# A second set of raw-weight buffers in the MLPs, half of it in large slots, and another order of the weight splits

## The chip, the cores and the metric

The kernel runs on one core of one Trainium2 chip. The metric is the device time of one execution in microseconds; each time given is the median of several executions on one chip. The engines are TensorE (PE), VectorE (DVE), ScalarE (ACT), GpSimd (POOL) and SyncE (SP), whose queue issues nearly all of this kernel's DMAs. Each engine takes its instructions in order.

## The reference

A trunk of two layers over 1024 positions with 1024 channels, all in fp32. Layer 0 mixes with a chunked gating MLP, layer 1 with dilated attention; each is followed by an MLP with squared ReLU, four times as wide. Cut to what matters here:

```
D_MODEL, SEQ, D_FF = 1024, 1024, 4 * 1024
h = x
for layer in range(2):
    y = _rms_norm(h, mix_norm_g[layer])
    y = _chunk_gating_mixer(y, ...) if layer == 0 else _dilated_attention_mixer(y, ...)
    h = h + y
    y = _rms_norm(h, mlp_norm_g[layer])
    h = h + jnp.square(jax.nn.relu(y @ w_up[layer])) @ w_down[layer]
return _rms_norm(h, final_norm_g)
```

## The kernel before

**Precision.** A matmul in fp32 is made of three in fp32r. Each operand is split into a high part (ACT copies it with rounding, line 203) and a low part (DVE subtracts, line 204), and PE adds hi × hi, hi × lo and lo × hi in one bank (`three`).

**Seven products for eight.** The large matrix products are cut into 2 × 2 blocks and done with seven products in place of eight. The weights of one such set are four raw quadrants of 128 × 512 (`Weights`, line 370). They are loaded by SP into buffers with the tag "r", of which there are four. POOL makes the sums (lines 389, 390, 391, 394), partly in place in the raws, and seven splits (ACT and DVE) write `wp` tiles, of which there are eight. Which product uses what: 4 uses r(1,1) raw, 1 uses r(0,0), 2 uses r(0,1); 5, 6, 7 and 3 use sums. Two sets are thus never raw at the same time: the loads of the next set wait until the splits of the set before have read its raws.

**Stages.** An MLP has an up stage of tiles q = 2 to 15 (q = 0 and 1 are computed in the classical way), and a down stage of tiles t = 0 to 17. In both, PE computes products in the order 5, 6, 1, 7, 3, 2, 4, and the weights of the next tile are split meanwhile: after each product the generator `more()` goes one step on. A full product is 12 matmuls of 512 columns (four blocks of 128 rows, three matmuls each). The first and last three tiles of the down stage have fewer blocks: tile 0 has one, tile 1 two, tile 2 three. The first set of an up stage (q = 2) and of the attention has no tile before it to hide in and is split at one go (line 712).

**Around it.** Up tiles put out hidden terms, which go to DRAM (`hid`, line 669). The down stage loads them again one tile ahead, in temporary tiles `t`, and splits them into `hx` pairs (`take`, `inputs`). DVE adds products to the state `h` (line 833) and to the partial sums `u` (lines 847, 856, 859), and in the up stage combines banks (lines 739, 746, 747, 755). A product that begins in a bank which an earlier one has used (3, 2 and 4 continue in the banks of 5, 1 and 7, new tiles take freed ones) waits for that.

**Slots.** A pool of 38 slots of 128 × 1024 words holds the state (8), and, depending on the stage, normed activations, hidden terms as pairs, or raw hidden terms. The last block of hidden terms is done in the classical way at the end of the down stage, with weights `we` and terms `xe` that are loaded and split during its last tiles (`ends`).

**Order.** PE's order is as written. On the other engines a list scheduler sets the order from the program order, dependencies and priorities (`tc.high_priority`), so the change of one buffer can move other instructions as well.

Of the kernel before, what the change touches and what calls it, by code (L numbers as in the profile page):

```python
# [10 lines left out]
F32 = mybir.dt.float32  # L11
# [6 lines left out]
P = 128  # L18
D = 1024
S = 1024  # L20
HALF = 512
# [91 lines left out]
def trunk(ctx: ExitStack, tc: tile.TileContext, xT, w_u, w_v, w_o, w_s, b_s, w_qkv, w_bo, rel,  # L113
# [14 lines left out]
    def temp():  # L128
        return tpool.tile([P, HALF], F32, tag="t", name="t", bufs=NT)
# [7 lines left out]
    def slot(shape=(P, S), dtype=F32, name="s"):  # L137

        return slots.tile(list(shape), dtype, tag="s", name=name)
# [21 lines left out]
    def raw():  # L161
        return tpool.tile([P, HALF], F32, tag="r", name="r", bufs=4)
# [10 lines left out]
    def mm_bank():  # L173
        return psm.tile([P, HALF], F32, tag="mm", name="mm")

    def at_bank():
        return psa.tile([P, HALF], F32, tag="at", name="at")
# [186 lines left out]
    def product(bank, w, xs, more=False):  # L364

        for k, x in enumerate(xs):
            three(bank, w, blk(k), x, not more and k == 0, k == len(xs) - 1, skip_group_check=True)
            flow.pump()

    class Weights:  # L370


# [11 lines left out]
        def steps(self):  # L384

            r, tt = self.r, nc.gpsimd.tensor_tensor
            self.split(4, r[1, 1])
            r3 = temp()[:, 0:r[0, 0].shape[1]]
            tt(r3, r[0, 0], r[1, 0], op=ALU.subtract)  # L389
            tt(r[1, 0], r[1, 0], r[1, 1], op=ALU.add)  # L390
            tt(r[1, 1], r[1, 0], r[0, 0], op=ALU.subtract)  # L391
            yield
            self.split(1, r[0, 0])
            tt(r[0, 0], r[0, 1], r[1, 1], op=ALU.subtract)  # L394
            yield
            for p, src in ((5, r[1, 0]), (6, r[1, 1]), (7, r3), (3, r[0, 0]), (2, r[0, 1])):
                self.split(p, src)
                yield

# [12 lines left out]
    def up(layer, q):  # L412
        return lambda i, j: w_up[layer, q, i, j]
# [276 lines left out]
    def mlp(layer, x, first, last):  # L690


        def up_weights(q):
            return Weights(up(layer, q))


        tiles = [(q, i) for q in range(2) for i in range(2)]
        c = {}
        for s in range(2):
            banks = [at_bank() if (n < 2) == (s == 1) else mm_bank() for n in range(4)]  # L700
            if s == 0:
                banks = [mm_bank() if n < 3 else at_bank() for n in range(4)]
            classical(x, first, s, banks)
            for b, (q, i) in zip(banks, tiles):
                c[q, i, s] = temp()
                with tc.high_priority(offset=PRIO):
                    squared(c[q, i, s], b)
                if s and i:
                    hidden_terms(q, c[q, 0, 0], c[q, 1, 0], c[q, 0, 1], c[q, 1, 1], c[q, 0, 0])
            if s == 0:  # L710
                w = up_weights(2)
                for _ in w.steps():
                    pass
        x.rest()

        for q in range(2, 16):
            down = Down(layer) if q == 15 else None
            wn = down.weights(0) if down else up_weights(q + 1)
            more = ahead(wn)
            more()  # L720
            d = at_bank()
            product(d, w[5], x.t[5])
            more()
            c22 = temp()
            nc.scalar.activation(c22, d, AF.Copy)  # L725
            if down:
                down.take(14, held, SEVEN[:4])
            b = at_bank()
            product(b, w[6], x.t[6])
            more()  # L730
            if down:
                down.take(14, held, SEVEN[4:])
            a = mm_bank()
            product(a, w[1], x.t[1])
            more()
            u = temp()
            with tc.high_priority(offset=PRIO):
                nc.scalar.activation(u, a, AF.Copy)  # L738
                nc.vector.tensor_tensor(u, u, b, op=ALU.add)
            if down:  # L740
                down.early(SEVEN[:4])
            e = at_bank()
            product(e, w[7], x.t[7])
            more()
            with tc.high_priority(offset=PRIO):
                nc.vector.tensor_tensor(c22, c22, e, op=ALU.add)  # L746
            nc.vector.tensor_tensor(c22, c22, u, op=ALU.add)
            squared(c22)
            if down:
                down.early(SEVEN[4:])  # L750
            product(d, w[3], x.t[3], True)
            more()
            c12 = temp()
            with tc.high_priority(offset=PRIO):
                nc.vector.tensor_tensor(c12, u, d, op=ALU.add)
            squared(c12)
            product(a, w[2], x.t[2], True)
            more()
            c11 = temp()
            squared(c11, a)  # L760
            product(e, w[4], x.t[4], True)
            more()
            c21 = temp()
            with tc.high_priority(offset=PRIO):
                nc.vector.tensor_tensor(c21, u, e, op=ALU.add)
            squared(c21)
            if q < 14:
                hidden_terms(q, c11, c21, c12, c22, u)
            elif q == 14:
                held = hidden_terms(q, c11, c21, c12, c22, u, False)  # L770
            else:
                kept(q, {(0, 0): c11, (1, 0): c21, (0, 1): c12, (1, 1): c22})
            w = wn
        down.run(w)
        down.close(last)

    class Down:
# [41 lines left out]
        def run(self, w):  # L819
            for t, (a, ks) in enumerate(self.todo):  # L820
                hs = {(i, s): h[a + 4 * i][:, half(s)] for i in range(2) for s in range(2)}
                wn = None
                if t < 17:
                    wn = self.weights(t + 1, **(dict(own=temp, place=pair) if t == 16 else {}))
                more = ahead(wn)
                more()

                def xs(p):
                    return [self.x[self.order[k]][p] for k in ks]

                def add(i, s, src, engine=nc.vector):
                    with tc.high_priority(offset=PRIO if engine is nc.vector else 0):
                        engine.tensor_tensor(hs[i, s], hs[i, s], src, op=ALU.add)  # L833

                if t == 16:
                    self.ends(0)
                d = at_bank()
                product(d, w[5], xs(5))
                more()
                add(1, 1, d)  # L840
                self.inputs(t + 1, (5,))
                b = at_bank()
                product(b, w[6], xs(6))
                more()
                if t >= 4:
                    with tc.high_priority(offset=PRIO):
                        nc.vector.tensor_tensor(self.u[a], self.u[a], b, op=ALU.add)
                self.inputs(t + 1, (6,))
                a_ = mm_bank()
                product(a_, w[1], xs(1))  # L850
                more()
                if t < 4:
                    self.u[a] = spare() if t < 2 else temp()
                    with tc.high_priority(offset=PRIO):
                        nc.scalar.activation(self.u[a], a_, AF.Copy)
                        nc.vector.tensor_tensor(self.u[a], self.u[a], b, op=ALU.add)
                else:
                    with tc.high_priority(offset=PRIO):
                        nc.vector.tensor_tensor(self.u[a], self.u[a], a_, op=ALU.add)  # L859
                self.inputs(t + 1, (1,))  # L860
                if t == 16:
                    self.ends(1)
                e = at_bank()
                product(e, w[7], xs(7))
                more()
                add(1, 1, e)
                self.inputs(t + 1, (7,))
                product(d, w[3], xs(3), True)
                more()
                add(0, 1, d)  # L870
                if t >= 14:
                    for i, s in ((1, 1), (0, 1)):
                        add(i, s, self.u[a], nc.gpsimd)
                self.inputs(t + 1, (3,))
                product(a_, w[2], xs(2), True)
                more()
                add(0, 0, a_)
                self.inputs(t + 1, (2,))
                product(e, w[4], xs(4), True)
                more()  # L880
                add(1, 0, e)
                if t >= 14:
                    add(1, 0, self.u[a], nc.gpsimd)
                self.inputs(t + 1, (4,))
                w = wn
# [531 lines left out]
    for n, two in enumerate(quads):  # L1417
        wn = Weights(qkv(*quads[n + 1])) if n + 1 < len(quads) else None
# [123 lines left out]
```

## Time and profile before

| | us |
|---|---|
| time, median of 3 runs | 2202.07 (2201.95 to 2205.04) |
| the profiled execution | 2201.35 |
| its span | 2199.6 |
| PE busy | 2129.9 |
| DVE busy | 1664.0 |
| ACT busy | 1132.7 |
| POOL busy | 608.3 |
| mean granted clock of PE | 0.987 |

The down stages run from about 626 to 930 and from about 1863 to 2170, the up stages from about 352 and 1592 on. A row of the timeline gives start, length, engine, line, operation, written and read tiles, shape and count; in brackets stands how long the engine was idle before it, and who ended that.

### The profile page before, as it was taken

What the parts mean: (1) busy time and instruction counts of PE and PEld (TensorE: products, weight loads), DVE (VectorE), ACT (ScalarE), POOL (GpSimd) and SP (SyncE); (2) the same over time, 40 slices, a digit from 0 to 9 for tenths busy, and PEclk for the clock granted to TensorE, in tenths of its full rate; (3) what the DMA queues carried; (4) which work ended last, traced back from release to release, by engine and by line L of the source; (5) the groups of instructions that cost most, each with busy time, mean ns of one, the idle gap of its engine ahead of it and who ended that gap; (6) DMA issues with size and microseconds to landing.
All of it is one profiled execution on the core that took longest, in us unless ns stands there. A gap on an engine that the chain in (4) does not pass through costs nothing.

```text
span 2199.6 us, 30242 instructions
## 1 busy us (share of the span) xinstructions
PE 2129.9 (97%) x10242; PEld 1758.3 (80%) x10242; DVE 1664.0 (76%) x2984; ACT 1132.7 (51%) x2294; POOL 608.3 (28%) x442
## 2 busy tenths in 40 slices
PE   7999999999999999998999999999989999999998
PEld 5888886888877888786888788887878888778887
DVE  6875259777788887788787877877887767888866
ACT  6744235555565444346665666664455556544433
POOL 1100114333323332443212222201333332332345
PEclk9999999999999999998999999999999999999999
DMA  6321113444444443321112111141044443554432
GB/s 221 100 83 48 48 41 112 157 151 151 151 163 162 158 157 120 110 82 45 45 42 46 42 53 42 46 161 47 29 168 153 154 148 128 175 166 152 151 110 77
DMA packets 155935, 241.81 MB, mean 110 GB/s; under 512 B 33161, under 2 KB 47620, under 8 KB 155780
## 3 DMA queue, kind: packets, MB, share of 16 engines
q1 hardware_dynamic: 154880, 238.65, 33.3%
q8 instruction: 80, 1.31, 0.3%
q10 hardware_dynamic: 900, 1.23, 0.2%
q14 instruction: 75, 0.61, 0.1%
HBM read 176.21 MB, written 63.61 MB: 109 GB/s over the span
## 4 chain that ended last, share of the span: by engine, by line
PE 76%; DVE 12%; issue 3%; ACT 3%; DMA 3%; POOL 1%; SPq 0%; DVEq 0%; POOLq 0%; ACTq 0%
PE mm L180 37%; PE at L180 37%; DVE wp L204 2%; DVE t L204 2%; PE at L187 2%; DMA r<-in_w_dn 1%; DVE y L204 1%; DMA t<-hid 1%; ACT t L1143 1%; ACT wp L203 1%; DVE h L833 1%; DVE q L1062 1%; DVE k L1062 1%; DVE tr L204 1%; DVE hx L204 1%
## 5 line engine op out<-in xcount | busy, mean ns | idle before, releaser
L203 ACT ACTIVATE wp<-r 128x512 fp32r<-128x512 f32 (+3 forms) x492 | 295.2, 604 | 352.2 <-PE at L180 165.1
L204 DVE TENSOR_TENSOR wp<-r,wp 128x512 fp32r<-128x512 f32 (+3 forms) x492 | 385.5, 787 | 76.2 <-ACT wp L203 73.6
L180 PE MATMUL at<-hx,wp 128*128 128x512 f32 x1770 | 414.4, 390 | 5.5 <-DVE h L833 2.8
L180 PE MATMUL mm<-y,wp 128*128 128x512 f32 x1608 | 404.6, 398 | 1.3 <-ACT t L738 0.8
L180 PEld LDWEIGHTS at<-hx,wp 128*128 128x128 f32 x1770 | 331.9, 188 | 77.0 <-DVE h L833 3.4
L389 POOL TENSOR_TENSOR t<-r 128x512 f32<-128x512 f32 (+3 forms) x78 | 110.3, 1414 | 907.3 <-DMA r<-in_w_up 281.5
L180 PEld LDWEIGHTS mm<-y,wp 128*128 128x128 f32 x1608 | 302.9, 191 | 68.2 <-ACT t L738 1.7
L180 PE MATMUL at<-t,wp 128*128 128x512 f32 x1344 | 318.7, 393 | 8.2 <-DVE t L746 8.2
L180 PEld LDWEIGHTS at<-t,wp 128*128 128x128 f32 x1344 | 255.2, 190 | 62.6 <-DVE t L746 9.0
L180 PE MATMUL mm<-t,wp 128*128 128x512 f32 x768 | 192.5, 397 | 2.3 <-DVE t L204 2.1
L180 PE MATMUL mm<-hx,wp 128*128 128x512 f32 x708 | 172.2, 390 | 5.6 <-DVE b L859 5.6
L261 POOL TENSOR_TENSOR t<-t 128x512 f32<-128x512 f32 (+1 forms) x54 | 69.1, 1279 | 385.4 <-ACT t L252 383.5
L204 DVE TENSOR_TENSOR hx<-t,hx 128x512 fp32r<-128x512 f32 x192 | 164.1, 870 | 11.7 <-ACT hx L203 11.6
L180 PEld LDWEIGHTS mm<-t,wp 128*128 128x128 f32 x768 | 141.5, 189 | 33.0 <-DVE t L204 2.5
L180 PEld LDWEIGHTS mm<-hx,wp 128*128 128x128 f32 x708 | 132.4, 188 | 34.9 <-ACT wp L203 5.0
L180 PE MATMUL mm<-y,whi 128*128 128x512 f32 x512 | 158.3, 390 | 0.0
L203 ACT ACTIVATE hx<-t 128x512 fp32r<-128x512 f32 x192 | 117.9, 627 | 52.5 <-DMA t<-hid 47.8
L180 PE MATMUL at<-y,wp 128*128 128x512 f32 x552 | 138.5, 392 | 3.0 <-ACT t L725 3.0
L833 DVE TENSOR_TENSOR h<-h,at 128x512 f32<-128x512 f32 x144 | 98.1, 683 | 51.6 <-PE at L180 50.5
L394 POOL TENSOR_TENSOR r<-r 128x512 f32<-128x512 f32 (+3 forms) x78 | 106.6, 1366 | 94.2 <-issue 77.3
L391 POOL TENSOR_TENSOR r<-r 128x512 f32<-128x512 f32 (+3 forms) x78 | 118.3, 1516 | 47.4 <-DVE wp L204 43.7
L180 PEld LDWEIGHTS at<-y,wp 128*128 128x128 f32 x552 | 103.7, 189 | 26.6 <-ACT t L725 3.8
(212 smaller groups left out, 3270.8 us busy)
## 6 DMA issues: line engine op xcount, KB each, us to landing
t<-hid SPq DMA_DIRECT2D x182, 256.0 KB, 4.6
hid<-t SPq DMA_DIRECT2D x140, 256.0 KB, 2.3
r<-in_w_up SPq DMA_DIRECT2D x128, 256.0 KB, 2.7
r<-in_w_dn SPq DMA_DIRECT2D x88, 256.0 KB, 2.6
r<-in_w_qkv SPq DMA_DIRECT2D x72, 256.0 KB, 2.7
hid<-b SPq DMA_DIRECT2D x56, 256.0 KB, 2.2
r<-in_w_v SPq DMA_DIRECT2D x48, 256.0 KB, 3.5
h<-in_xT SPq DMA_DIRECT2D x16, 256.0 KB, 4.3
```

Of the source, the lines that this page charges most:

```text
L180: nc.tensor.matmul(out, lhsT, rhs, **kw)
L187: nc.tensor.transpose(out, src, ident)
L203: nc.scalar.activation(hi, src, AF.Copy)
L204: nc.vector.tensor_tensor(lo, src, hi.bitcast(F32), op=ALU.subtract)
L261: nc.gpsimd.tensor_tensor(self.acc, self.acc, sq, op=ALU.add)
L389: tt(r3, r[0, 0], r[1, 0], op=ALU.subtract)
L391: tt(r[1, 1], r[1, 0], r[0, 0], op=ALU.subtract)
L394: tt(r[0, 0], r[0, 1], r[1, 1], op=ALU.subtract)
L833: engine.tensor_tensor(hs[i, s], hs[i, s], src, op=ALU.add)
L1062: nc.vector.scalar_tensor_tensor(lo, a, sc, hi.bitcast(F32), op0=ALU.mult, op1=ALU.subtract)
L1143: nc.scalar.activation(p[:, c], p[:, c], AF.Exp, bias=m, scale=-1.0, accum_out=dn)
```

## The change

In `Weights` an allocator `own` can be given. `mixed()` is a new one: of the four raws of a set it places two, (1,1) and (0,1), in "r" buffers as before, and two, (1,0) and (0,0), in the halves of one slot with the tag "r2". All sets of the up stage from q = 4 on and all sets of the down stage from t = 1 on use it, except the last (t = 17), which has temporary tiles before and now. So two sets fit the four "r" buffers. And product 2, whose raw quadrant needs no sum, is split third and not last: 4, 1, 2, 5, 6, 7, 3 in place of 4, 1, 5, 6, 7, 3, 2, in all sets, the attention's among them.

```
+    def mixed():
+        got = []
+        def one():
+            if not got:
+                two = slot((P, 2, HALF), F32, "r2")
+                got.extend([raw(), two[:, 1, :], raw(), two[:, 0, :]])
+            return got.pop()
+        return one
...
-            for p, src in ((5, r[1, 0]), (6, r[1, 1]), (7, r3), (3, r[0, 0]), (2, r[0, 1])):
+            for p, src in ((2, r[0, 1]), (5, r[1, 0]), (6, r[1, 1]), (7, r3), (3, r[0, 0])):
...
         def up_weights(q):
-            return Weights(up(layer, q))
+            return Weights(up(layer, q), own=mixed() if q > 3 else None)
...
-                    wn = self.weights(t + 1, **(dict(own=temp, place=pair) if t == 16 else {}))
+                    wn = self.weights(t + 1, **(dict(own=temp, place=pair) if t == 16 else dict(own=mixed())))
```

Behind these lines the numbers of the changed kernel are 12 higher (lines 833 and 859 become 845 and 871).

**Place 1: DVE, the first set of layer 0's up stage.** Rows are line, operation, written tile and what is read. The four raws are r_2996 (1,0), r_2998 (1,1), r_3000 (0,0) and r_3002 (0,1); t_3007 is the sum that product 7 reads. Before, the first rows are products 4, 1, 5 and 6:

```order
L204 TENSOR_TENSOR wp_3004<-r_2998,wp_3004 128x512
L204 TENSOR_TENSOR wp_3011<-r_3000,wp_3011 128x512
L204 TENSOR_TENSOR wp_3015<-r_2996,wp_3015 128x512
L204 TENSOR_TENSOR t2_3151<-b_3128,t2_3151 128x512
L204 TENSOR_TENSOR wp_3018<-r_2998,wp_3018 128x512
```

and now 4, 1, 2 and 5:

```order
L204 TENSOR_TENSOR wp_3004<-r_2998,wp_3004 128x512
L204 TENSOR_TENSOR wp_3011<-r_3000,wp_3011 128x512
L204 TENSOR_TENSOR wp_3015<-r_3002,wp_3015 128x512
L204 TENSOR_TENSOR t2_3151<-b_3128,t2_3151 128x512
L204 TENSOR_TENSOR wp_3018<-r_2996,wp_3018 128x512
```

Twelve rows later, behind the splits of the activations, DVE had products 7, 3 and 2:

```order
L204 TENSOR_TENSOR t4_3265<-keep_2730,t4_3265 128x512
L204 TENSOR_TENSOR t3_3270<-keep_2749,t3_3270 128x512
L204 TENSOR_TENSOR wp_3021<-t_3007,wp_3021 128x512
L204 TENSOR_TENSOR wp_3024<-r_3000,wp_3024 128x512
L204 TENSOR_TENSOR wp_3027<-r_3002,wp_3027 128x512
```

and now has 6, 7 and 3:

```order
L204 TENSOR_TENSOR t4_3265<-keep_2730,t4_3265 128x512
L204 TENSOR_TENSOR t3_3270<-keep_2749,t3_3270 128x512
L204 TENSOR_TENSOR wp_3021<-r_2998,wp_3021 128x512
L204 TENSOR_TENSOR wp_3024<-t_3007,wp_3024 128x512
L204 TENSOR_TENSOR wp_3027<-r_3000,wp_3027 128x512
```

The split of product 6 has moved from the first group to the second. The attention's first set and layer 1's up stage move in the same way.

**Place 2: the start of layer 0's down stage, DVE and SP.** On DVE, from the split of tile 1's product 4 (wp_5583 before) to that of its product 6 (wp_5610). The raws of tile 1 before are r_5571 (1,0), r_5574 (1,1), r_5577 (0,0) and r_5580 (0,1):

```order
L204 TENSOR_TENSOR wp_5583<-r_5574,wp_5583 128x256
L833 TENSOR_TENSOR h4_96<-h4_96,at_5590 128x512
L204 TENSOR_TENSOR wp_5594<-r_5577,wp_5594 128x256
L204 TENSOR_TENSOR wp_5603<-r_5571,wp_5603 128x256
L833 TENSOR_TENSOR h4_96<-h4_96,at_5616 128x512
L856 TENSOR_TENSOR b_5613<-b_5613,at_5599 128x512
L833 TENSOR_TENSOR h0_92<-h0_92,at_5590 128x512
L833 TENSOR_TENSOR h0_92<-h0_92,mm_5606 128x512
L833 TENSOR_TENSOR h4_96<-h4_96,at_5616 128x512
L204 TENSOR_TENSOR wp_5610<-r_5574,wp_5610 128x256
```

Now r2_5559 is the slot with (1,0) and (0,0), r_5561 is (1,1), r_5560 is (0,1):

```order
L204 TENSOR_TENSOR wp_5570<-r_5561,wp_5570 128x256
L845 TENSOR_TENSOR h4_96<-h4_96,at_5577 128x512
L204 TENSOR_TENSOR wp_5581<-r2_5559,wp_5581 128x256
L845 TENSOR_TENSOR h4_96<-h4_96,at_5603 128x512
L868 TENSOR_TENSOR b_5600<-b_5600,at_5586 128x512
L845 TENSOR_TENSOR h0_92<-h0_92,at_5577 128x512
L845 TENSOR_TENSOR h0_92<-h0_92,mm_5593 128x512
L845 TENSOR_TENSOR h4_96<-h4_96,at_5603 128x512
L204 TENSOR_TENSOR wp_5590<-r_5560,wp_5590 128x256
L204 TENSOR_TENSOR wp_5597<-r2_5559,wp_5597 128x256
L204 TENSOR_TENSOR wp_5607<-r_5561,wp_5607 128x256
```

The split of product 5 (from wp_5603 to wp_5597) has moved from before the adds of tile 0 to behind them. On SP, somewhat later, the raws of tile 3 and the hidden terms of its block stood so:

```order
L169 DMA r<-in_w_dn 128x384
L169 DMA r<-in_w_dn 128x128
L169 DMA r<-in_w_dn 128x384
L169 DMA t<-hid_5_3427 128x512
L169 DMA t<-hid_6_3434 128x512
```

and now:

```order
L169 DMA r<-in_w_dn 128x512
L169 DMA r_5755<-in_w_dn 128x128
L169 DMA r_5755<-in_w_dn 128x384
L169 DMA r_5755<-in_w_dn 128x128
L169 DMA r_5755<-in_w_dn 128x384
L169 DMA r<-in_w_dn 128x512
L169 DMA t<-hid_5_3427 128x512
L169 DMA t<-hid_6_3434 128x512
```

Half of the raws ahead of the hidden terms (r_5755, the slot) now need no "r" buffer, and the other half has one free a set earlier.

**Place 3: DVE near the end of layer 0's down stage.** Before, the `we` tiles stood in tile 15 (128x256 splits are those of tile 16):

```order
L204 TENSOR_TENSOR wp_7894<-r_7854,wp_7894 128x256
L204 TENSOR_TENSOR we_7980<-t_7981,we_7980 128x512
L204 TENSOR_TENSOR we_7985<-t_7986,we_7985 128x512
L859 TENSOR_TENSOR t_5992<-t_5992,mm_7898 128x512
L204 TENSOR_TENSOR wp_7908<-r_7856,wp_7908 128x256
```

and now they stand in tile 14 (128x384 splits are those of tile 15):

```order
L871 TENSOR_TENSOR t_5824<-t_5824,mm_7745 128x512
L204 TENSOR_TENSOR we_7952<-t_7953,we_7952 128x512
L204 TENSOR_TENSOR wp_7758<-r2_7696,wp_7758 128x384
L204 TENSOR_TENSOR we_7957<-t_7958,we_7957 128x512
L845 TENSOR_TENSOR h6_98<-h6_98,at_7762 128x512
```

They have moved one tile earlier, and the `xe` tiles and the splits of the last set with them.

## The prediction

> **What bounds the kernel now.** I read the page's busy shares first, then stretches of the span (the windows view), then the timeline of the engine that waits in each stretch.
>
> ```profile
> PE 2129.9 (97%) x10242; PEld 1758.3 (80%) x10242; DVE 1664.0 (76%) x2984; ACT 1132.7 (51%) x2294; POOL 608.3 (28%) x442
> ```
>
> TensorE (PE) is busy for 97% of the span of 2199.6 us, so about 70 us are all that any reordering can touch. The windows view says where. Its columns are the stretch, its length, then busy time of PE, PEld, DVE, ACT and POOL, the granted clock, and two DMA columns.
>
> ```profile
> 378.49:381.90 3.41, 3.41 (x9) 2.67 (x8) 1.90 (x4) 2.70 (x5) 0.00 (x0) 0.50 0.45 152
> 400.00:600.00 200.00, 200.00 (x884) 165.60 (x884) 142.97 (x168) 104.75 (x178) 66.71 (x44) 1.00 0.47 154
> 640.00:700.00 60.00, 55.23 (x240) 44.50 (x240) 52.12 (x76) 30.60 (x57) 22.84 (x16) 1.00 0.56 187
> 910.00:925.00 15.00, 11.91 (x51) 8.95 (x50) 15.00 (x25) 3.85 (x7) 6.76 (x5) 0.99 0.48 152
> 921.21:924.62 3.41, 1.74 (x8) 1.00 (x7) 3.41 (x7) 0.00 (x0) 1.31 (x2) 1.00 0.39 117
> 924.62:928.03 3.41, 3.41 (x10) 2.65 (x9) 1.86 (x3) 0.00 (x0) 3.25 (x3) 0.50 0.18 62
> 1614.11:1620.94 6.83, 5.84 (x14) 4.64 (x15) 4.72 (x8) 4.56 (x9) 0.00 (x0) 0.50 0.59 197
> 1880.00:1940.00 60.00, 55.40 (x240) 44.42 (x239) 51.14 (x76) 30.57 (x56) 22.10 (x16) 1.00 0.54 180
> ```
>
> In the middle of the up stage (400 to 600) PE has no idle time at all: 884 matmuls in 200 us, 226 ns each, so a product of 12 matmuls is 2.72 us. Raw weights that arrive earlier cannot make that faster. The loss sits at the seams: the first 60 us after tile 1 of the down stage (60.00 − 55.23 = 4.77 us in layer 0, 60.00 − 55.40 = 4.60 in layer 1), the end of layer 0's down stage (15.00 − 11.91 = 3.09), and the starts of the up stages. Some seams are followed by a period at clock 0.50: 3.41 us long at 378.49 and 924.62, 6.83 at 1614.11. A period of 3.41 at half clock gives 1.7 us less work. The starts lie on one grid: (924.62 − 378.49) / 160 = 3.413. A stretch that was half idle was enough: PE was busy 1.74 of 3.41 us in 921.21 to 924.62, and the next stretch ran at 0.50.
>
> The Trainium skill, page "TensorE: Matmul & The Clock Gate", section "What's actually happening", has a free-running window of 3413 ns, which fits that grid, but puts the slow state after at least one idle window; the trace disagrees there, since the window before 924.62 was half busy. By the page's rule the half clock in the fourth term below would not come, and the sum would be 1.7 us better.
>
> **The change, part by part.** It adds no instruction and no byte; it moves loads (SP's queue) and splits (ACT and DVE). Products run on PE in an unchanged order (5, 6, 1, 7, 3, 2, 4).
>
> **1. The up stages' first set, about −3.0 us (bounds +3 and −4.6).** This set of weights is split at one go, so only the new order matters to it.
>
> ```profile
> 355.47 5.60 PE L180 MATMUL at<-t,wp 128*128 128x512 f32 x24
> ...
> 377.95 4.36 PE L180 MATMUL at<-t,wp 128*128 128x512 f32 x11 [4.10 <-DVE t L746]
> ```
> ```profile
> 351.66 0.68 DVE L204 TENSOR_TENSOR wp<-r,wp 128x512 fp32r<-128x512 f32 x1
> ...
> 360.29 1.87 DVE L204 TENSOR_TENSOR t<-keep,t 128x512 fp32r<-128x512 f32 x3
> 362.09 0.67 DVE L204 TENSOR_TENSOR wp<-t,wp 128x512 fp32r<-128x512 f32 x1
> ...
> 377.21 0.68 DVE L746 TENSOR_TENSOR t<-t,at 128x512 f32<-128x512 f32 x1
> ```
>
> The 24 matmuls are products 5 and 6, so PE reaches product 6 at 355.47 + 2.72 = 358.19. Its split is the row at 351.66. After the change product 2 and 5 stand before it, and it falls into the place that product 7's has now, 362.09, ready at 362.76: PE waits 4.57 us. But the stage's last product (4) starts only at 377.95, when the add of line 746 frees its bank, and that add stands at the same place on DVE as before. Products 6, 1, 7, 3 and 2 need 5 × 2.72 = 13.6 us: 362.76 + 13.6 = 376.4, before 377.95. So the wait is moved, not added. What may go is the half clock behind it: 1.7 us at 378.49 and, in layer 1, 6.83 × 0.5 less the idle 1 us = 2.9 us.
>
> ```profile
> 1591.82 5.15 PE L180 MATMUL at<-t,wp 128*128 128x512 f32 x22
> ...
> 1615.10 7.10 PE L180 MATMUL at<-t,wp 128*128 128x512 f32 x18 [4.11 <-DVE t L746]
> ```
> ```profile
> 1594.59 4.71 DVE L204 TENSOR_TENSOR t<-keep,t 128x512 fp32r<-128x512 f32 x7
> ```
>
> In layer 1 product 6 is reached at 1591.82 + 10 × 0.226 = 1594.1 and split after the row of seven, at 1594.59 + 4.71 + 0.6 = 1599.9, a wait of 5.8; 1599.9 + 13.6 = 1613.5, plus up to 1.7 for a half clock in the new place, stands against 1615.10. Gains are 1.7 + 2.9 = 4.6 at most; I take 3.0, because a new wait may call up a half clock of its own. The other end, +3, is two such periods that are not absorbed.
>
> **2. The down stages' start, −9.0 us (bounds 0 and −9.4).**
>
> ```profile
> 678.29 8.45 PE L180 MATMUL at<-hx,wp 128*128 128x512 f32 x36 [1.20 <-DVE h L833]
> ...
> 697.13 3.00 PE L180 MATMUL mm<-hx,wp 128*128 128x512 f32 x12 [2.22 <-DVE b L859]
> ```
> ```profile
> 677.70 7.95 SPq L169 DMA_DIRECT2D r<-in_w_dn  x3
> 685.70 3.27 SPq L169 DMA_DIRECT2D t<-hid  x7
> ```
> ```profile
> 689.56 0.91 DVE L204 TENSOR_TENSOR hx<-t,hx 128x512 fp32r<-128x512 f32 x1 [2.16 <-ACT hx L203]
> ```
> ```profile
> SPq L169 <- DVE wp L204: 925.1, 314, 41.3
> ```
>
> Read from the end: PE waits for DVE's adds (lines 833, 859); DVE, which takes its work in order, stood still for 2.16 us behind a hidden term; that term's load left SP only at 685.70, because SP had been held for 7.95 us on three raw weights that had no free buffer. Such waits for a raw buffer are the largest of SP's queue, 925.1 us in 314 times, mostly harmless. With two sets of buffers the raws do not hold the queue here and the hidden terms go out some 7 us earlier, more than DVE's 2.16. Both layers: 4.77 + 4.60 = 9.4; I take 9.0 because each small wait of the two stretches must go. If something else holds DVE the gain is nothing.
>
> **3. The end of layer 0's down stage, −4.0 us (bounds 0 and −4.8).**
>
> ```profile
> 915.74 1.63 PE L180 MATMUL mm<-hx,wp 128*128 128x512 f32 x6 [1.41 <-DVE b L859]
> ```
> ```profile
> 876.97 0.69 DVE L833 TENSOR_TENSOR h<-h,at 128x512 f32<-128x512 f32 x1 [1.56 <-PE at L180]
> ```
>
> DVE is full from 910 to 925 (15.00 of 15.00), and PE waits 3.09 us for its adds, followed by the half clock at 924.62 (1.7). Some 40 us earlier DVE idles 1.56 us between adds. In the new order the splits of the last set and of the `we` and `xe` tiles stand a tile earlier, in those holes. Together 4.8; a little will stay, since the attention's first weights are split between the adds of the last two tiles as before.
>
> **4. Tile 1 of the down stage, +5.7 us (bounds 0 and +7.4).**
>
> ```profile
> 634.13 3.59 PE L180 MATMUL at<-hx,wp 128*128 128x512 f32 x15
> ```
> ```profile
> 630.10 0.69 DVE L765 TENSOR_TENSOR t<-t,at 128x512 f32<-128x512 f32 x1 [2.08 <-PE at L180]
> ...
> 635.34 0.68 DVE L833 TENSOR_TENSOR h<-h,at 128x512 f32<-128x512 f32 x1
> 635.94 0.42 DVE L204 TENSOR_TENSOR wp<-r,wp 128x256 fp32r<-128x256 f32 x1
> ```
>
> Tile 0 has one block, so its products are 3 matmuls, 0.68 us, and four products of lead are no longer 11 us but 2.7. The 15 matmuls are tile 0's last product and tile 1's first two; product 5 of tile 1 starts at 634.8. Its split stood ahead of tile 0's adds; now it stands behind the add at 635.34 and behind product 2's: 635.94 + 0.47 + 0.42 = 636.8. PE waits 2.0 us, in both layers 4.0, and I add one half clock (1.7; both would be 3.4). Nothing is lost if ACT and DVE catch up in the 2.08 us that DVE has before this tile.
>
> **5. The attention's first set, +2.9 us (bounds +0.2 and +5.6).**
>
> ```profile
> 996.75 2.82 PE L180 MATMUL mm<-t,wp 128*128 128x512 f32 x10
> 1001.71 0.73 PE L180 MATMUL mm<-t,wp 128*128 128x512 f32 x2 [2.15 <-DVE t L204]
> 1006.97 1.11 PE L187 MATMUL at<-ident,t 128*128 128x128 f32 x4 [4.53 <-ACT t L1019]
> ```
> ```profile
> 1006.54 0.68 DVE L204 TENSOR_TENSOR wp<-t,wp 128x512 fp32r<-128x512 f32 x1
> ```
>
> Here product 6 is the first. Its split moves behind the seven splits of the last activations, to the place at 1006.54, ready at 1007.2. The product's 2.72 us, which lay ahead of the wait that ends at 1006.97, come after it: 1007.2 + 2.72 − 6.97 − 1000 = 2.9. At half clock they take twice as long (5.6); if what follows is late anyway, 0.2.
>
> **6. The steady tiles, 0.** Each split comes one product later, still four products (4 × 2.72 = 10.9 us) ahead of its use, with DVE busy 142.97 of 200. This cover is what hides the new order; each microsecond beyond it would cost one per tile.
>
> **Sum:** −3.0 − 9.0 − 4.0 + 5.7 + 2.9 = −7.4 us. The profiled execution took 2201.35 us, so 2194.0 there; the median of the runs shown is 0.7 higher (2202.07), which gives **2194.7**, said as 2194.5.
>
> **The rivals.**
>
> **The down start is bound by DVE, not by the loads.** For it: DVE is 52.12 of 60 us busy in 640 to 700, its shares are averages, and POOL works 22.84 us beside it. Against: 1.20 and 2.22 us of PE's wait stand next to 2.16 us in which DVE did nothing. Half of term 2 would stay: −7.4 + 4.5 = −2.9, 2199.2, no change that a measurement tells.
>
> **Slower: the late product 6 is not absorbed.** If the add of line 746 slips with its product, both waits of term 1 are added: 4.57 + 5.8 = 10.4 instead of −3.0. Then −7.4 + 13.4 = +6.0, 2208.1. Each microsecond by which that add starts later than 377.21 (and its like in layer 1) is one of time, and at 7.4 in the two layers together the gain is gone. For it: in layer 1 the slack is 1.6 us (1615.10 − 1613.5). Against: in between DVE waits for nothing from PE.
>
> **The change does not do what it says.** The large slots are shared with the hidden terms; if none is free, the second set waits for a slot as it waited for a buffer. Terms 2 and 3 fall away and −3.0 + 5.7 + 2.9 = +5.6 stays: 2207.7. For it: of 38 slots 8 hold the state and up to 28 the hidden terms of four blocks. Against: there each tile's terms are freed seven at a time.
>
> **How the numbers follow.** Forecast 0.62, DVE-bound 0.22, product 6 not absorbed 0.09, no slots 0.07. A measurement of this kernel tells 0.2% from no change, 4.4 us: faster is below 2197.7, slower above 2206.5. Of the forecast 0.59 lies below and 0.03 within; of the DVE case 0.05 and 0.17; of the last two, which centre just above the upper bound, 0.07 within and 0.09 above. Faster 0.64, same 0.27, slower 0.09. With all terms at their good ends (4.6 + 9.4 + 4.8 − 0.2 = 18.6) the time is 2183.5; at their bad ends (+3 + 7.4 + 5.6 = 16) it is 2218. The range of 8 in 10 is 2185 to 2207, which leaves out half of the slower cases and the extreme ends.
>
> **What would show it.** Right: in 640 to 700 and 1880 to 1940 PE is busy over 59 of 60; SP issues the hidden terms of tile 4 before 680; 910 to 925 shows under 1 us idle and no half clock behind it. New waits on ACT or DVE's `wp`: 4 to 6 us at about 358 and 1594, 2 us at about 635 and 1873, 10 us at 997. Wrong: PE's waits for lines 833 and 859 stay at the down start; the add of line 746 comes later than 378 and 1615; or a wait inside 400 to 600, where term 6 says none.

## The result, and the profile after

| | us |
|---|---|
| before, median of 4 runs | 2203.56 (2201.95 to 2207.61) |
| after, median of 4 runs | 2190.48 (2188.81 to 2192.09) |
| ratio after / before | 0.9938, 95% interval 0.9922 to 0.9954 |
| profiled execution, before and after | 2201.35 and 2188.81 |
| its span, before and after | 2199.6 and 2187.1 |

The change makes the kernel 0.6% faster, 13.1 us between the medians and 12.5 us between the two profiled executions. The windows of the changed kernel, with the same columns as before:

```profile
400.00:600.00 200.00, 200.00 (x884) 165.62 (x883) 129.93 (x169) 106.53 (x180) 60.69 (x42) 1.00 0.45 151
640.00:700.00 60.00, 58.81 (x259) 48.22 (x259) 57.14 (x76) 31.60 (x56) 20.76 (x14) 1.00 0.52 170
900.00:925.00 25.00, 24.64 (x108) 19.81 (x107) 23.51 (x37) 7.89 (x15) 13.48 (x9) 1.00 0.35 105
1865.51:1868.92 3.41, 3.41 (x10) 2.65 (x9) 3.08 (x7) 2.02 (x4) 1.77 (x2) 0.50 0.99 347
1880.00:1940.00 60.00, 59.60 (x262) 48.71 (x261) 54.97 (x73) 29.53 (x51) 20.72 (x14) 1.00 0.47 157
```

The steady tiles (400 to 600) are full, as they were. The starts of the down stages have 1.19 and 0.40 us idle in place of 4.77 and 4.60, the end of layer 0's down stage 0.36 in place of 3.09. In their place stand waits that were not there. Their rows, from PE's timeline:

```profile
362.29 0.74 PE L180 MATMUL at<-t,wp 128*128 128x512 f32 x2 [1.65 <-ACT wp L203]
365.18 4.63 PE L180 MATMUL at<-t,wp 128*128 128x512 f32 x10 [2.15 <-DVE wp L204]
...
380.92 3.34 PE L180 MATMUL at<-t,wp 128*128 128x512 f32 x14
```
```profile
638.56 2.58 PE L180 MATMUL at<-hx,wp 128*128 128x512 f32 x10 [2.03 <-DVE wp L204]
```
```profile
661.37 3.01 PE L180 MATMUL at<-hx,wp 128*128 128x512 f32 x12 [1.19 <-DVE h L845]
```
```profile
1865.04 4.15 PE L180 MATMUL at<-hx,wp 128*128 128x512 f32 x10 [1.90 <-DVE wp L204]
```
```profile
997.72 1.22 PE L180 MATMUL mm<-t,wp 128*128 128x512 f32 x2 [6.41 <-ACT wp L203]
1001.75 4.23 PE L180 MATMUL mm<-t,wp 128*128 128x512 f32 x10 [2.82 <-DVE wp L204]
```

All but the one at 661.37 name a weight split: the tile's first products (6, 5 and 6) wait for `wp`. The one at 661.37 is a wait for an add of DVE, in front of a product that did not wait before. At the up stage's start the last product (380.92) now starts with no wait of its own; the 4.10 us that stood there are gone.

Both programs have the same 10242 matmuls in the same order, so the start of one matmul can be compared with the start of the same matmul in the other trace, and the difference can be cut into stretches. The table gives how much longer a stretch took than in the profile before (us; minus is shorter), for the change and for four of the experiments below ("4th run" and "6th run" count the experiments in their order).

| stretch (time in the kernel before) | after | order only | buffers only | 4th run | 6th run |
|---|---|---|---|---|---|
| up to 39 | +2.3 | +2.9 | +1.9 | +2.5 | +1.9 |
| rest of the gating layer, to 357 | 0.0 | +1.6 | +1.6 | +1.6 | +1.4 |
| layer 0, start of the up stage, to 410 | −1.0 | −1.2 | 0.0 | −1.3 | −1.5 |
| up stage, to 633 | 0.0 | +0.1 | 0.0 | 0.0 | 0.0 |
| tile 1 of the down stage, to 644 | +2.2 | +1.0 | +2.8 | −0.1 | −0.1 |
| start of the down stage, to 711 | −4.4 | −3.0 | −3.7 | −3.8 | −4.4 |
| its middle, to 912 | 0.0 | 0.0 | 0.0 | 0.0 | 0.0 |
| its end, to 934 | −4.6 | −1.6 | −4.6 | −4.6 | −4.6 |
| attention's first set, 996 to 1022 | +2.0 | +1.9 | 0.0 | 0.0 | +1.6 |
| rest of the attention, to 1553 | −2.4 | −1.6 | −1.7 | +1.0 | −5.7 |
| to 1593 | −1.6 | −1.6 | 0.0 | −1.6 | −0.1 |
| layer 1, start of the up stage, to 1637 | −2.8 | −1.8 | 0.0 | −2.8 | −2.8 |
| up stage, to 1872 | −0.1 | +0.4 | −0.1 | −0.1 | −0.1 |
| tile 1 of the down stage, to 1883 | +3.8 | +1.3 | +1.9 | 0.0 | 0.0 |
| start of the down stage, to 1947 | −5.0 | −3.3 | −3.6 | −0.2 | −4.7 |
| rest | −0.6 | −0.6 | −0.7 | −0.6 | −0.6 |
| sum | −12.3 | −5.5 | −6.2 | −9.9 | −19.6 |

One profile is one execution, and an execution has scatter of its own: the 17 runs of the kernel before in the first set of experiments reach from 2197.07 to 2205.98. The table shows where it sits. In the first 39 us each trace of the table is 1.9 to 2.9 us behind the profile before, with nothing changed there. In the rest of the attention the fourth, fifth and sixth runs, whose instruction orders differ only at the up stages' start and around tile 4 of the down stages, stand at +1.0, −3.8 and −5.7. Most of that goes with the half clock, of which their traces have 23.9, 17.1 and 10.2 us in this stretch. The −2.4 of the changed kernel lies inside this scatter and can't be put down to the change. The down stages' middles agree within 0.01 us.

### The profile page after: what moved, and what is told of

Its sections match the earlier page's. It is cut to its first block, busy times and chain, and to the rows that moved or that the text cites. A ratio compares the mean times of both kernels' runs of the same rounds, so it can differ in the third digit from the quotient of the medians.

```text
span 2187.1 us, 30151 instructions
## 1 busy us (share of the span) xinstructions
PE 2125.1 (97%) x10242; PEld 1756.1 (80%) x10242; DVE 1661.2 (76%) x2984; ACT 1135.4 (52%) x2294; POOL 594.8 (27%) x442
## 4 chain that ended last, share of the span: by engine, by line
PE 82%; DVE 10%; ACT 3%; issue 2%; DMA 2%; SPq 0%; DVEq 0%; ACTq 0%
PE at L180 41%; PE mm L180 39%; PE at L187 2%; DVE wp L204 2%; DVE t L204 2%; DVE h L845 1%; DVE hx L204 1%; ACT t L1155 1%; DMA r<-in_w_up 1%; DVE y L204 1%; DMA h<-in_xT 1%; DVE k L1074 0%; DMA t<-hid 0%; DVE tr L204 0%; DMA r<-in_w_v 0%
## 5 line engine op out<-in xcount | busy, mean ns | idle before, releaser
L401 POOL TENSOR_TENSOR t<-r 128x512 f32<-128x512 f32 (+3 forms) x78 | 101.1, 1297 | 634.7 <-DMA r<-in_w_dn 277.0
L204 DVE TENSOR_TENSOR hx<-t,hx 128x512 fp32r<-128x512 f32 x192 | 181.6, 959 | 6.5 <-ACT hx L203 6.5
```

Source lines behind the costliest of these rows:

```text
L204: nc.vector.tensor_tensor(lo, src, hi.bitcast(F32), op=ALU.subtract)
```

## The experiments

**The new order alone.** The second set of buffers is taken back.

```
-            return Weights(up(layer, q), own=mixed() if q > 3 else None)
+            return Weights(up(layer, q))
...
-    ... if t == 16 else dict(own=mixed())))
+    ... if t == 16 else {}))
```

> Only the new order of the splits; raw buffers as before. Theory (the seams' gain comes from the second set of buffers): the waits in 640 to 700 and 1880 to 1940 stay near 4.7 us each and the 3.1 us at the end of layer 0's down stage stay; tile 1 of the down stage waits about 2 us in both layers and the attention's first set costs 1.6 to 2.9, the up stages' starts give 3 back: 2202 to 2207 us. Rival (the order alone frees r(0,1) early, so that one raw of the next set can be loaded ahead): half of the waits at the down starts go, 2197 to 2201 us.

Measured: 2195.33 us against 2202.04, ratio 0.9965 (0.9951 to 0.9978). This is below both ranges, on the rival's side; the theory's is missed. The table has it by stretch: the starts of the down stages lose 3.0 and 3.3 us of waits with the old buffers. What goes is seen in what DVE waits for in the 60 us from 640 on. Before:

```profile
DVE wp L204 <- ACT wp L203: 4.7, 6, 1.8
DVE hx L204 <- ACT hx L203: 3.1, 3, 2.2
```

and with the new order alone:

```profile
DVE hx L204 <- ACT hx L203: 2.9, 4, 1.6
DVE wp L204 <- ACT wp L203: 1.3, 1, 1.3
```

(columns: waiting operation, what it waited for, us in total, times, longest). The waits on weights fall from 4.7 to 1.3 us, those on hidden terms stay. In 3.5 of the 4.7 us (0.87, 0.17, 0.66 and 1.83) the ACT copy that DVE waited for had itself waited for POOL's sums, on lines 390 and 391. The split of product 5, which needs such a sum, used to stand where now a split stands that needs none. The rival expected this gain from a raw that is loaded ahead; what the rows show is only that the weights' waits shrink. Tile 1 waits 0.75 and 1.05 us, less than the 2 expected, and tile 2, which did not wait before, 0.90 and 0.81 us at its start; the −3.0 and −3.3 are net of the latter.

**The second set of buffers alone,** splits in the old order.

```
-            for p, src in ((2, r[0, 1]), (5, r[1, 0]), (6, r[1, 1]), (7, r3), (3, r[0, 0])):
+            for p, src in ((5, r[1, 0]), (6, r[1, 1]), (7, r3), (3, r[0, 0]), (2, r[0, 1])):
```

> Only the second set of buffers; splits in the old order. Theory: the waits at the down starts (9.4 us) and at layer 0's down end (3.1, with its half clock) go as in the changed kernel, the up stages' and the attention's first sets are as before; tile 1 of the down stage still waits 1.6 us in both layers, because its product 5 stands behind tile 0's adds on DVE here too: 2193 to 2196 us. Rival (the gain needs the early split of product 2): the down starts keep half of their waits, 2198 to 2201 us.

Measured: 2192.33 us, ratio 0.9951 (0.9936 to 0.9966), a little under the theory's range. By stretch the starts of the down stages lose 3.7 and 3.6 us, their end 4.6, the first sets are as before (0.0 in three places), and tile 1 waits in both layers, 1.52 and 1.56 us. So the end of layer 0's down stage belongs to the buffers: with them PE's waits there fall from 3.09 to 0.41 us, with the order alone 2.88 stay. (The −1.6 of the order alone is the half clock, which is missing there too in the next run, with 3.26 us of waits and neither part of the change.) The start of the down stage belongs to either part: of the 9.4 us that both take together the order alone takes 6.3 and the buffers alone 7.3. The wait at tile 1, too, comes with either part alone. In 640 to 700 this run's DVE no longer waits for hidden terms, but 5.7 us for weights, the reverse of the run before.

**Hidden terms on another queue,** in the kernel before: ACT and not SP issues their loads in the down stage.

```
-                self.take(k, {p: load(hidden_tile(k, p), temp()) for p in which}, which)
+                self.take(k, {p: load(hidden_tile(k, p), temp(), nc.scalar) for p in which}, which)
```

> The kernel before, but the loads of the hidden terms in the down stage are issued by ACT, not by SP. Theory (what was late at the down start are hidden terms held on SP's queue behind raws that wait for a buffer): PE is idle under 2 us in the stretch of layer 0 that was 640 to 700 and in that of layer 1, tile 1 has no wait, 2194 to 2197 us. Rival (the raws themselves, or DVE's amount of work, are late): more than 3 us stay idle in each stretch, 2200 to 2205 us.

Measured: 2198.06 us, ratio 0.9984 (0.9974 to 0.9995), between the two. PE's idle time in the two stretches, 2.4 and 3.2 us, misses the theory's too. The waits of before on lines 833 and 859 are gone from both layers, and DVE's waits in 640 to 700 fall from 4.7 and 3.1 us to

```profile
DVE wp L204 <- ACT wp L203: 1.1, 2, 0.9
DVE hx L204 <- ACT hx L203: 0.9, 2, 0.6
```

In their place PE waits for a copy on ACT; one row of each layer:

```profile
661.26 2.33 PE L180 MATMUL mm<-hx,wp 128*128 128x512 f32 x9 [1.42 <-ACT t L855]
```
```profile
1893.35 3.21 PE L180 MATMUL mm<-hx,wp 128*128 128x512 f32 x8 [2.21 <-ACT t L855]
```

That copy stood on ACT behind splits that waited for hidden terms to land (15.3 us of ACT's idle time in 640 to 700, 9.5 in the kernel before). So with another queue for the hidden terms no second set of buffers is needed to remove the waits on lines 833 and 859. The run does not tell late hidden terms from late weights, though: SP's queue then holds the raws alone, and both of DVE's waits shrink. The way round costs about half of what it gains: the two stretches are shorter by 2.9 and 0.6 us, where the waits on lines 833 and 859 were 3.4 and 3.3.

**Without the waits at tile 1 and at the attention's start.** The attention's first set and tile 1 of the down stages are split in the old order, and tile 1's raws lie in "r" buffers.

```
-            for p, src in ((2, r[0, 1]), (5, r[1, 0]), ...
+            rest = [(5, r[1, 0]), (6, r[1, 1]), (7, r3), (3, r[0, 0])]
+            rest.insert(4 if self.old else 0, (2, r[0, 1]))
...
+    ... else dict(own=mixed() if t else None, old=t == 0)
...
+            w = Weights(qkv(*quads[0]), old=True)
```

> The changed kernel, but the attention's first set and tile 1 of the down stage are split in the old order, and tile 1's raws lie in the old buffers. Theory: no wait at tile 1 (5.1 us won against the changed kernel) and 1.6 to 2.9 won at the attention's start, the rest as in the changed kernel: 2182 to 2185 us. Rival (the adds of tile 0 and the split of product 5 share DVE's time, so that the wait only moves to tile 2): 2187 to 2190 us.

Measured: 2186.1 us, ratio 0.9928 (0.9914 to 0.9942), between theory and rival. The interval overlaps that of the changed kernel (0.9922 to 0.9954), so what was won is read from the traces. The three waits are gone: −0.1 and 0.0 at tile 1, 0.0 at the attention's first set. But in layer 1 the wait came back 60 us later:

```profile
1924.46 3.92 PE L180 MATMUL mm<-hx,wp 128*128 128x512 f32 x9 [2.32 <-DVE b L873]
```

The stretch there is −0.2 us, where the changed kernel has −5.0: PE arrives earlier at the tile whose hidden terms are late, and waits for them. In the changed kernel too SP holds those loads; layer 1, from SP's queue:

```profile
1890.17 0.90 SPq L169 DMA_DIRECT2D t<-hid  x2
1902.33 0.33 SPq L169 DMA_DIRECT2D r<-in_w_dn  x1
1902.70 2.33 SPq L169 DMA_DIRECT2D t<-hid  x5
```

Five of the seven loads of tile 4 stand behind one raw weight that gets its buffer only at 1902.33, some 11 us after the row before it.

**The up stages' start in the old order.** The fourth run, with the first sets of the up stages in the old order as well.

```
-            return Weights(up(layer, q), own=mixed() if q > 3 else None)
+            return Weights(up(layer, q), own=mixed() if q > 3 else None, old=q == 2)
```

> As the fourth run (attention's first set and tile 1 in the old order, tile 1 with the old buffers), but the first sets of both up stages are split in the old order too. Theory (the new order at the up stages' start only moves PE's wait ahead, and so spares a half clock behind it): PE waits again in front of product 4, 4 us in each layer, with a half clock behind it, and the time is 3 to 4 us above the fourth run's 2186.1: 2189 to 2190 us. Rival (the order of the first set makes no difference to the end of the stage's start): 2185 to 2187 us.

Measured: 2188.0 us, ratio 0.9937 (0.9924 to 0.9949), between theory and rival, and on another chip than the fourth run's. Against the fourth run's 0.9928 the intervals overlap, so the times decide nothing; the traces show the mechanism. PE waits again in front of product 4:

```profile
381.09 3.23 PE L180 MATMUL at<-t,wp 128*128 128x512 f32 x7 [4.84 <-DVE t L760]
```

and half clock follows it, 3.41 us at 381.26; in layer 1 the wait is 4.73 us. By stretch the starts of the up stages are 0.0 and −1.4 us, against −1.3 and −2.8 in the fourth run: the new order is worth 1.3 and 1.4 us there, less than the expected 3 to 4 in all.

**Tile 4's hidden terms on ACT's queue.** The fourth run, with these seven loads in each layer issued by ACT.

```
+                self.take(k, {p: load(hidden_tile(k, p), temp(), nc.scalar if t == 4 else None) for p in which}, which)
```

> As the fourth run, but ACT issues the loads of tile 4's hidden terms (seven in each layer), which SP held for about 11 us behind a raw weight. Theory (these loads set DVE's and so PE's wait at 1887 and 1924): the waits on lines 847 and 873 that the fourth run kept (0.84 and 0.74 in layer 0, 1.20 and 2.32 in layer 1) go, 2180 to 2183 us. Rival (ACT, which takes its work in order, holds back what follows): a wait of 1.4 us or more on ACT's copy appears in each layer, 2185 to 2188 us.

Measured: 2182.55 us against 2202.71, ratio 0.9913 (0.9899 to 0.9926), in the theory's range. The waits on line 873 are gone in both layers; one wait on line 847 stays in each:

```profile
1881.69 7.80 PE L180 MATMUL at<-hx,wp 128*128 128x512 f32 x33 [0.94 <-DVE h L847]
```

In layer 0 it is 1.24 us. No wait of PE on ACT's copy appears. The starts of the down stages are −4.4 and −4.7 us, with nothing given back at tile 1. This version has the lowest time of all, though its interval overlaps the fourth run's; a part of its −19.6 us in the table (−5.7) is the attention's scatter.

**Buffers in the down stages alone, and in the up stages alone.**

```
-            return Weights(up(layer, q), own=mixed() if q > 3 else None)
+            return Weights(up(layer, q))
```

> The changed kernel with the second set of buffers in the down stages alone; the up stages use the old four. Theory (PE never waits in the steady up tiles, so raws that arrive earlier there are worth nothing): as the changed kernel, 2189 to 2192 us, and 400 to 600 without idle time in both. Rival (the up stage's buffers also bring the down stage's first sets forward): 2193 to 2196 us.

Measured: 2190.9 us, ratio 0.9950 (0.9937 to 0.9962), as the changed kernel (2190.48, 0.9938). The other half:

```
-    ... if t == 16 else dict(own=mixed())))
+    ... if t == 16 else {}))
```

> The changed kernel with the second set of buffers in the up stages alone; the down stages use the old four. Theory: as the run with the new order alone, 2194 to 2197 us, half of the waits at the down starts and the 3 us at layer 0's down end stay. Rival (the up stages' buffers carry a part of the gain): 2190 to 2193 us.

Measured: 2196.43 us, ratio 0.9974 (0.9964 to 0.9983), as the new order alone (2195.33): 2.2 and 3.4 us idle stay at the down starts and 2.7 at layer 0's down end. The up stages' second set of buffers is worth nothing that can be measured.

## Why the prediction was right

The time was 2190.48 us against the forecast 2194.5, inside the range, and every term has the sign and about the size that was forecast. In terms 1 and 2, however, most of the gain came by a path that the prediction had not seen, so that the sizes agree there is in part luck. By its steps, from the two profiles:

| term | predicted | measured |
|---|---|---|
| 1, start of the up stages | −3.0 | −3.8 (−1.0 and −2.8) |
| 2, start of the down stages | −9.0 | −9.4 (−4.4 and −5.0) |
| 3, end of layer 0's down stage | −4.0 | −4.6 |
| 4, tile 1 of the down stages | +5.7 | +6.0 (+2.2 and +3.8) |
| 5, the attention's first set | +2.9 | +2.0 |
| 6, steady tiles | 0 | 0.0 |
| sum | −7.4 | −9.8 |

**Term 1**: the wait moved as described, but the gain came in another way. PE waits 1.65 + 2.15 = 3.80 us in front of product 6, 0.8 less than the 4.57 worked out: two matmuls need only the high part, and started while DVE still worked on the low one. In layer 1 it waits 3.37 + 1.21 = 4.58 us in place of 5.8. Product 4 then starts without a wait. The prediction took its gain from the half clock that might go. It did not go: it now comes at 363.64 and at 1589.03, 6.83 us each, where it was 3.41 and 6.83 long. There it runs in part into idle time:

```profile
363.64:370.47 6.83, 5.29 (x13) 4.13 (x14) 6.66 (x10) 6.22 (x13) 1.38 (x2) 0.50 0.58 174
```

What shrank is PE's idle time, from 5.41 to 3.80 us in layer 0's stretch (before: 0.83, 0.49 and 4.10) and from 6.57 to 4.58 in layer 1's. That the new order wins something here all traces bear out: the six with it have −1.0 to −1.5 and −1.8 to −2.8 us in these two stretches, the three with the old order 0.0 in layer 0, and 0.0, −0.2 and −1.4 in layer 1.

**Term 2** had the right size and half of the reason. The prediction put the whole of it on raws that hold SP's queue in front of the hidden terms. In the kernel before, DVE also stood still for 4.7 us on weights, most of it on sums that were not there, and this it left out. The first of PE's two waits for DVE, at 678.29, follows on such a stop of DVE, not on a hidden term; from here to the add of line 833 DVE has no other idle time:

```profile
672.90 1.23 DVE L204 TENSOR_TENSOR wp<-r,wp 128x512 fp32r<-128x512 f32 x1 [1.83 <-ACT wp L203]
```
```profile
672.24 0.63 ACT L203 ACTIVATE wp<-r 128x512 fp32r<-128x512 f32 x1 [2.98 <-POOL r L390]
```

The changed kernel shows which of the two went. Its 640 to 700 have one row of DVE's waits left:

```profile
DVE hx L204 <- ACT hx L203: 2.9, 2, 2.3
```

The waits for weights are gone, those for hidden terms are what they were (3.1 before); layer 1 is alike (5.8 to 0, and 3.0 to 3.7, in 1880 to 1940 before and 1870 to 1930 now). Nor did the raws cease to hold SP's queue. From 655 to 692 it waited for their buffers, before and after:

```profile
SPq L169 <- DVE wp L204: 28.8, 9, 6.2
```
```profile
SPq L169 <- DVE wp L204: 31.6, 5, 10.1
```

The seven loads that left at 685.70 leave at 682.30, 3.4 us earlier and not 7 (5.0 if one takes off that this trace is 1.6 us behind there). So, as I read it, PE's waits went because DVE, without the stops for weights, had time to spare for the same stops for hidden terms. Late hidden terms are a cause all the same: with the buffers alone DVE's waits for them go and its waits for weights stay, and the start of the down stage still gains 7.3 us; with the order alone it is the other way round, and 6.3. I read the two as one queue, DVE's, in which the time won from one wait covers a part of the other; no run shows that by itself.

**Term 3** is the buffers' work: −4.6 with them alone. With the order alone nearly all of the waits stay.

**Term 4** was forecast as 2.0 us in each layer with one half clock in all; waits of 2.03 and 1.90 us came, and the half clock in layer 1. That it agrees to the tenth is luck: PE reaches product 5 at 635.24 + 3 × 0.226 = 635.92 and goes on behind the split at 638.56, 2.6 us later, but two matmuls that need only the high part ran in between. What the prediction read from the order, that product 5's split stood behind tile 0's adds and product 2's, fits the runs: with tile 1 in the old order and the old buffers the wait is gone. It did not see that either part of the change alone is enough to put it there.

**Term 5** was 0.9 too large. The product's 12 matmuls did come behind the split (997.72, 1001.75), but the first two ran ahead of the low part here too, and the transposes that waited 4.53 us behind an ACT copy before follow the product without a wait (at 1005.82). That the new order of the first set costs this is borne out by its four traces with the new order, +1.7 to +3.1, against 0.0 in four with the old one; a fifth with the old one, the sixth run's, has +1.6, with a half clock of 13.6 us there in place of 10.2 in the fourth run's, so the size is known to about 1.5 us only.

**What is left:** −12.3 less −9.8 is −2.5 us, in stretches that the change does not touch in any way the traces show: +2.3 at the start, −2.4 and −1.6 in and behind the attention, and −0.8 in small ones. The first and the attention's scatter by as much between executions with the same instructions there, as the table shows. So of the 4.9 us between −7.4 and −12.3 about half are terms taken on the cautious side, and half is scatter between two profiled executions.

**The signs that it named** came in part. From 900 to 925 PE idles 0.36 us and no half clock follows. PE is busy 59.60 of 60 us at layer 1's down start, but 58.81, just under the 59 named, at layer 0's. The new waits are 3.8 us at 362 and 4.6 at 1590 (4 to 6 named), 2.0 and 1.9 at tile 1 (2 named) and 9.2 at 997 (10 named). The add of line 746 comes at 379.61, later than 378, which was named as a sign of being wrong; but 2.3 of the 2.4 us more the trace brings along from its first 39 us. The hidden terms of tile 4 left SP at 664.39 and 675.81, before 680, and that shows nothing: in the kernel before they left at 668.04 and 674.58. The row at 685.70 that the sign goes back to is tile 5's. (In the sixth run, where ACT loads tile 4's, the group of two and five is the one missing from SP's queue.)

**The rivals.** That DVE's amount of work bounds the down start, so that half of term 2 stays, is refuted by the −9.4, and in layer 1 by the rows too (0.40 us idle are left, DVE busy 54.97 of 60). In layer 0, with 57.14 of 60, there is hardly room: from 640 to 677 DVE is never idle, and the new wait of 1.19 us for its add on line 845 falls there. Product 6 was absorbed. The slots did not hold the loads up: with the buffers alone DVE's waits for hidden terms went.

## What to carry to other kernels

Where the bound engine is 97% busy, the gain of more buffers is at the seams only, where tiles are short or a stage begins; the same buffers in the steady tiles were worth nothing. Splits that need no sum go ahead of those that do where an in-order engine would stand still, but not in a short tile or in the attention's first set, where the first product's own operand must come first; in the first sets of the up stages, whose last product waits for a bank anyhow, the new order won. And what is won at one seam is kept only if the next late transfer is moved as well: here two small follow-ups, the old order for the attention's first set and for tile 1, and seven loads on another queue, took the ratio from 0.9938 to 0.9913 (the intervals, 0.9922 to 0.9954 and 0.9899 to 0.9926, just overlap).

## What the hardware showed that was not expected

The half clock does not need an idle stretch of the grid, nor does the idle share of one stretch alone always decide it. Before the period at 1865.51 PE was busy 1.51 of 3.41 us, and half clock followed; on the same grid (1865.51 − 363.64 = 440 × 3.413) PE was busy 1.55 us in 636.70 to 640.11, and full clock followed:

```profile
636.70:640.11 3.41, 1.55 (x7) 1.29 (x8) 3.41 (x8) 1.59 (x4) 1.11 (x2) 1.00 0.98 329
640.11:643.52 3.41, 3.41 (x17) 2.80 (x16) 3.41 (x5) 3.20 (x8) 2.36 (x2) 1.00 0.93 331
```

In the kernel before, 1.74 us busy were little enough for half clock at 924.62. All ten traces together leave only a narrow band open. Outside the attention (from 30 to 990 and from 1560 to 2165), I take the stretches of each trace's grid that ran at full clock. The 27 in which PE was busy for at most 1.52 us were all followed by half clock; of those with more than 1.75 us, 122 of them under 3.3, none was; of the 11 between, five were. So here the limit lies near half a stretch. In the attention (1000 to 1555) 21 stretches with 1.75 to 2.7 us, and eight in which PE was busy throughout, were followed by half clock too. What decides there, and between 1.52 and 1.75 us, stays open; no run was made for it. The rule that the prediction quoted from the Trainium skill, page "TensorE: Matmul & The Clock Gate", section "What's actually happening", that a whole idle window must come before, does not hold here: 1.51 of 3.41 us busy was enough in this trace.
